# State space operators of a hybrid layer: products and splits taken from GpSimd to VectorE, and u computed three blocks ahead

## The chip, the cores and the metric

The kernel runs on one core of a Trainium2 chip. The core has a matrix engine (TensorE, PE in the profile, with its weight loads as PEld), a vector engine (VectorE, DVE), a scalar engine (ScalarE, ACT), a general engine (GpSimd, POOL) and an engine that here only issues transfers (SyncE, SP). Each engine takes its instructions in the order of its own queue. The metric is the device time of one execution in microseconds; before the change the median of three runs is 1744.01 us.

## What is computed

The layer has a sequence of 1024 tokens behind 16 meta tokens, width 1024. Cut to what matters here:

```
xn = rmsnorm(h);  q, k, v, u, g_att, g_ssm = split(xn @ w_in)
attn = sliding_window_attention(norm(q), norm(k), v)       # 16 heads, 4 kv heads
y = s5_ssm(u, ...)     # 64 groups of 16 channels, 64 complex states each
ssm = za * sigmoid(zb),  za, zb = split(gelu(y) @ w_glu)
h = h + merge(attn, ssm) @ w_out;  h = h + swiglu(rmsnorm(h))
```

The state space branch works in chunks of T = 8 steps. Per block of 8 groups it needs two operator tables of 128 x 1024 numbers, each a complex product of a power of the state matrix with an input or an output matrix: `bp = GR*XB + GI*YB` and `cp = AR*XC + AI*YC`. The matrix products with fp32 accuracy run in three passes: each weight tile is split into a rounded high part and a rest (`lw = raw - hi`).

## The kernel before

**Norm and k, v.** Eight blocks of x (and the meta tokens) are normed (`norm_T`), transposed and split; the reciprocal root is a chain of 13 small VectorE instructions (`rsqrt`, lines 146 to 160). Then k and v are projected, and k is scaled by its norm (line 287, nine products on GpSimd).

**Small chain.** VectorE computes powers of the state matrix on 128 x 64 tables (AR, AI, GR, GI), lines 305 to 388.

**u.** `u_block(f)` (line 400) projects 128 channels of u: the weight tile is loaded by SyncE, rounded by ScalarE (line 103), its rest is taken by GpSimd (line 104), and TensorE makes three products of 272, 256 and 512 columns with 24 matmuls each. A product's PSUM bank is copied out by ScalarE (272 and 512 columns) or VectorE (256 columns, line 407). Eight transfers write u to memory, and `ut` (line 483) reads it back in another layout.

**Operators.** The loop at line 448 takes eight blocks. Each makes bp and cp (lines 460 to 463: first product on GpSimd into the one buffer `tmp`, second product and sum on VectorE; all three are called `ops` in the trace), writes cp out, multiplies bp into `kl`, transposes it into `bpt`, calls `u_block(blk + 1)`, reads `ut`, multiplies it with `bpt` into `v`, copies that into `vs` and lets `step` (line 187, ten VectorE instructions a block, shown as cm and vs) combine neighbouring chunks. XB, YB, XC and YC come from eight transposes of b and c (`bcT`, line 434) that stand behind `u_block(0)`. XB uses the buffer of the small chain's `t12`.

**After it.** Four gate units (`g_unit`, line 526, 24 matmuls each; their weights are split by `w_cols` on GpSimd) and the attention follow. The attention's buffers take the memory that the operators' pool `pp` gives back, the gates' `sg` that of `po`, whose first buffer is YC. The order within each engine's queue is not the written one: a planner simulates the program with its own costs and puts down, at each point, the first written instruction that is ready by its reckoning.

Of the kernel before, what the change touches and what calls it, by code (L numbers as in the profile page):

```python
# [8 lines left out]
F32 = mybir.dt.float32  # L9
F32R = mybir.dt.float32r  # L10
I32 = mybir.dt.int32
BF16 = mybir.dt.bfloat16
AF = mybir.ActivationFunctionType
ALU = mybir.AluOpType
# [3 lines left out]
P = 128  # L18
# [5 lines left out]
HD = 64  # L24
NQ = 16
NKV = 4
# [4 lines left out]
EPS = 1e-6  # L31
# [15 lines left out]
def hybrid_layer_kernel(ctx: ExitStack, tc: tile.TileContext, x, meta_tokens, norm_mix, w_in, q_norm, k_norm,  # L47
                        attn_sinks, lam_re, lam_im, log_dt, ssm_b_re, ssm_b_im, ssm_c_re, ssm_c_im, ssm_d,
                        w_glu, attn_branch_norm, ssm_branch_norm, w_out, norm_ffn, w_ffn_in, w_ffn_out, out):
    nc = tc.nc  # L50
    x, out = x[0], out[0]
# [55 lines left out]
    def w_cols(w, c0, n, name, lo=None, pools=(pool_r,)):  # L107

        per = 1024 // n
        parts = []  # L110
        for i in range(KB // per):
            src = w[i * per * P:(i + 1) * per * P, c0:c0 + n].rearrange("(a p) n -> p a n", p=P)
            parts.append(w_tile(src, (per, n), f"{name}_{i}", lo, pools[i % len(pools)]))
        return lambda kb, part: parts[kb // per][part][:, kb % per, :]
# [31 lines left out]
    def rsqrt(ms, rows, n, pool, name):  # L146

        def t(nm, dt=F32):
            return pool.tile([P, n], dt, tag=f"rs_{nm}{n}", name=f"rs_{nm}_{name}")[:rows]
        xe, xh, q, i = t("xe"), t("xh"), t("q"), t("i", I32)  # L150
        nc.vector.tensor_scalar(out=xe, in0=ms, scalar1=EPS, scalar2=None, op0=ALU.add)
        nc.vector.tensor_scalar(out=xh, in0=ms, scalar1=EPS, scalar2=-0.5, op0=ALU.add, op1=ALU.mult)
        nc.vector.tensor_scalar(out=i, in0=xe.bitcast(I32), scalar1=1, scalar2=None, op0=ALU.logical_shift_right)
        nc.vector.tensor_scalar(out=i, in0=i, scalar1=-1.0, scalar2=float(0x5F3759DF), op0=ALU.mult, op1=ALU.add)
        y = i.bitcast(F32)
        for _ in range(3):
            nc.vector.tensor_tensor(out=q, in0=y, in1=y, op=ALU.mult)
            nc.vector.tensor_tensor(out=q, in0=q, in1=xh, op=ALU.mult)
            nc.vector.scalar_tensor_tensor(out=y, in0=q, scalar=1.5, in1=y, op0=ALU.add, op1=ALU.mult)
        return y  # L160

    def norm_T(src, rows, gain, emit, pool, name, bufs=2):


        ss = pool.tile([P, 1], F32, tag="ss", name=f"ss_{name}")
        xs = pool.tile([P, D], F32, tag="xs", bufs=bufs, name=f"xs_{name}")
        nc.scalar.activation(out=xs[:rows], in_=src[:rows], func=AF.Square, scale=1.0 / 32, accum_out=ss[:rows])
        r = rsqrt(ss[:rows], rows, 1, pool, name)
        nc.vector.scalar_tensor_tensor(out=xs[:rows], in0=src[:rows], scalar=r, in1=gain[:rows],
                                       op0=ALU.mult, op1=ALU.mult)  # L170
        for i in range(2):
            pt = bank(f"nt_{name}_{i}", "x")
            for k in range(4):
                nc.tensor.transpose(pt[:, k * P:k * P + rows], xs[:rows, (4 * i + k) * P:(4 * i + k + 1) * P],
                                    ident[:rows, :rows])
            emit(i, pt.rearrange("p (k n) -> p k n", k=4)[:, :, :rows])
# [37 lines left out]
    with sbuf("p1", 2) as p1:  # L214
# [34 lines left out]
        dt = sm("dt")  # L249
# [34 lines left out]
        kr = rsqrt(kss.rearrange("p b h -> p (b h)"), P, 36, p1, "k").rearrange("p (b h) -> p b h", b=9)  # L284
        for b, (k, n) in enumerate([(ks[:, b, :], P) for b in range(8)] + [(ksm, NMETA)]):
            k = k.rearrange("p (h d) -> p h d", d=HD)
            nc.gpsimd.tensor_tensor(out=k, in0=k, in1=kr[:n, b].unsqueeze(2).to_broadcast([n, NKV, HD]), op=ALU.mult)

        nc.vector.memset(vm.bitcast(F32), 0.0)
        split(vm[0:16, :, 0], vm[0:16, :, 1], o[:NMETA, 256:512].rearrange("p (h d) -> p h d", d=HD))  # L290
# [2 lines left out]
        def tt(o, a, b, op=ALU.mult, eng=None):  # L293
            (eng or nc.vector).tensor_tensor(out=o, in0=a, in1=b, op=op)  # L294
# [31 lines left out]
        dt = sh  # L326
# [63 lines left out]

    def xn_cols(w, c0, name, emit):

        wt = w_cols(w, c0, P, name)
        for h, off, n in ((0, 0, 272), (0, 272, 256), (1, 0, 512)):
            o = bank(f"{name}_{h}_{off}")
            mm3(o[:, :n], wt, lambda kb, part: xn[h][part][:, kb, off:off + n], KB)
            emit(o[:, :n], off + 528 * h, n)

    with sbuf("pp", 1) as pp:
        def u_block(f):  # L400
            uf = pp.tile([P, T, NCH], F32, tag="uf", bufs=2, name=f"uf{f}")

            def emit(o, c0, n):
                dst = uf.rearrange("p t n -> p n t")[:, c0 // T:(c0 + n) // T, :]
                src = o.rearrange("p (n t) -> p n t", t=T)
                if n == 256:
                    nc.vector.tensor_copy(dst, src)  # L407
                else:
                    nc.scalar.copy(dst, src)
            xn_cols(w_in, CU + f * P, f"u{f}", emit)  # L410
            for t in range(T):
                nc.sync.dma_start(out=u_d[f, :, t], in_=uf[:, t, :])
# [8 lines left out]
        nc.gpsimd.memset(zrows, 0.0)  # L421
        nc.gpsimd.dma_start(out=kl_d[8:15].rearrange("s c g e -> (s c) (g e)"), in_=zrows)

        u_block(0)

        XB, YB, XC, YC = (po.tile([P, 16, GRP], F32, tag=n, name=n) for n in ("XB", "YB", "XC", "YC"))
        for what in range(2):
            raw = bc[what][:GRP].rearrange("g a b -> g (a b)")
            X, Y = ((XB, YB), (XC, YC))[what]
            for hh in range(2):  # L430
# [6 lines left out]
                def half(v):  # L437
# [4 lines left out]
                                        scalar2=None, op0=ALU.mult)  # L442
        ops = [pp.tile([P, 2, D], F32, tag="bc", bufs=2, name=f"ops{i}") for i in range(2)]
        bp, cp = (ops[0][:, i].rearrange("p (g s c) -> p g s c", g=8, s=8) for i in range(2))
        tmp = ops[1][:, 0].rearrange("p (g s c) -> p g s c", g=8, s=8)
        bpts = ops[1][:, 1], pp.tile([P, D], F32, tag="bpt", name="bpt1")
        SH = [P, 8, 8, 16]
        for blk in range(8):
            g0 = blk * 8
            bpt = bpts[blk % 2]  # L450

            def gs(v):
                return v[:, :, g0:g0 + 8].rearrange("p s g -> p g s").unsqueeze(3).to_broadcast(SH)

            def cs(v):
                return v[:, :, g0:g0 + 8].rearrange("p c g -> p g c").unsqueeze(2).to_broadcast(SH)

            dd = pp.tile([P, P], F32, tag="dd", name=f"dd{blk}")
            nc.scalar.dma_start(out=dd, in_=ssm_d[0:1, g0 * 16:g0 * 16 + P].to_broadcast([P, P]))
            for o, (p1_, q1), (p2_, q2) in ((bp, (GR, XB), (GI, YB)), (cp, (AR, XC), (AI, YC))):  # L460
                tt(tmp, gs(p1_), cs(q1), eng=nc.gpsimd)
                tt(o, gs(p2_), cs(q2))
                tt(o, o, tmp, ALU.add)
            nc.sync.dma_start(out=cp_d[blk], in_=cp.rearrange("p g t c -> p (g t c)"))
            kl = bank(f"kl{blk}", "x")
            for g in range(8):
                nc.tensor.matmul(kl[:, g * 16:g * 16 + 16], bp[:, g].rearrange("p s c -> p (s c)"),
                                 XC[:, :, g0 + g], start=True, stop=True)
            for hh in range(2):
                pt = bank(f"bpT{blk}{hh}", "x")  # L470
                for g in range(4):
                    nc.tensor.transpose(pt[:, g * P:g * P + P], bp[:, hh * 4 + g].rearrange("p s c -> p (s c)"), ident)
                nc.scalar.copy(bpt[:, hh * 512:hh * 512 + 512], pt)
            kls = pp.tile([P, 8, 16], F32, tag="kls", bufs=2, name=f"kls{blk}")
            tt(kls, dd.rearrange("p (g c) -> p g c", c=16),
               ident[:, 112:128].unsqueeze(1).to_broadcast([P, 8, 16]))
            tt(kls, kls, kl[:, 0:128].rearrange("p (g c) -> p g c", c=16), ALU.add)
            nc.sync.dma_start(out=kl_d[0:8, :, g0:g0 + 8, :].rearrange("s c g e -> (s c) g e"), in_=kls)
            if blk < 7:
                u_block(blk + 1)  # L480

            ut = pp.tile([P, 8, NCH], F32, tag="ut", bufs=2, name=f"utv{blk}")
            nc.sync.dma_start(out=ut, in_=u_d[blk].rearrange("g t c n -> (t c) g n"))
            vs = pp.tile([P, 2, 4, NCH], F32, tag="vs", bufs=2, name=f"vs{blk}")
            for e in range(2):
                for j in range(2):
                    o = bank(f"v{blk}{e}{j}", "q" if j else "x")
                    for k in range(2):
                        g = e + 4 * j + 2 * k
                        nc.tensor.matmul(o[:, k * NCH:(k + 1) * NCH], bpt[:, g * P:g * P + P], ut[:, g, :],  # L490
                                         start=True, stop=True)
                    for ri in range(2):
                        nc.scalar.copy(vs[64 * e:64 * e + 64, ri, 2 * j:2 * j + 2, :],
                                       o[64 * ri:64 * ri + 64, 0:2 * NCH].rearrange("p (k n) -> p k n", k=2))


            step(vs[:, :, :, 1::2], vs[:, :, :, 0::2], a8, 4 * blk, pp)
            step(vs[:, :, :, 5::4], vs[:, :, :, 3::4], a16, 4 * blk, pp)
            nc.sync.dma_start(out=v_d[:, :, 4 * blk:4 * blk + 4, :], in_=vs)
# [268 lines left out]
    for c in range(5, NCH - 1, 4):  # L768
        s1 = W[:, :, :, c]
        nc.vector.tensor_tensor(out=m, in0=W[:, :, :, c - 4].unsqueeze(1).to_broadcast([P, 2, 2, GRP // 2]),  # L770
                                in1=a32.rearrange("p (k r) g -> p k r g", k=2), op=ALU.mult)
# [508 lines left out]
```

## Time and profile before

| | |
|---|---|
| median of 3 runs (lowest, highest) | 1744.01 us (1743.16, 1745.96) |
| profiled execution, time | 1743.45 us |
| profiled execution, span of the trace | 1741.7 us |
| mean granted TensorE clock | 0.959 of full speed |
| busy: PE, DVE, ACT, POOL | 1599.2, 1203.1, 692.3, 510.1 us |

The span runs from the first to the last instruction, and the execution's time is 1.75 us longer. Busy shares are means over the whole span; the stage that the change touches lies between 70 and 286 us of it.

### The profile page before, as it was taken

The page shows a single profiled execution, that of the slowest core. Times are in us where ns is not written, and L with a number is a line of the kernel's source. Part 1 is how long each engine was busy: PE and PEld are TensorE (multiplying, and loading weights), DVE is VectorE, ACT ScalarE, POOL GpSimd, SP SyncE. Part 2 cuts the span into 40 slices and gives each one's busy share as a digit, 9 for nine tenths or more (in the row PEclk, how much of TensorE's full clock was granted, in tenths as well). Part 3 has the DMA queues.
Part 4 walks back from the last instruction along what each step waited for, and adds up shares of the span by engine and source line. Part 5 has one row for each costly group of instructions (what it writes and reads, how often), then busy time and mean ns, then how long its engine had stood idle before and what let it go on. Part 6 is the DMA issues. An engine that isn't in the chain of part 4 may idle for free.

```text
span 1741.7 us, 22246 instructions
## 1 busy us (share of the span) xinstructions
PE 1599.2 (92%) x8002; PEld 1331.6 (76%) x8002; DVE 1203.1 (69%) x2247; ACT 692.3 (40%) x1355; POOL 510.1 (29%) x345
## 2 busy tenths in 40 slices
PE   7968899989989968889999798799999999799998
PEld 5767788868767857788888687688888888678887
DVE  7779983899996699552114768966665556299763
ACT  4323233888886311153222332533333333244330
POOL 0245431333242523401332400012111111256541
PEclk9988899999999988989999999899999999999999
DMA  5153443110111853492221343233333222395432
GB/s 185 46 112 107 133 147 102 31 38 27 36 49 46 288 159 97 128 272 67 73 73 55 120 152 116 73 121 107 100 109 103 91 92 79 128 348 182 145 111 78
DMA packets 175358, 196.93 MB, mean 113 GB/s; under 512 B 12768, under 2 KB 125408, under 8 KB 175120
## 3 DMA queue, kind: packets, MB, share of 16 engines
q1 hardware_dynamic: 166736, 183.94, 32.8%
q10 hardware_dynamic: 8288, 11.01, 2.0%
q8 instruction: 63, 1.03, 0.3%
q0 software_dynamic: 224, 0.56, 0.1%
q14 instruction: 47, 0.39, 0.1%
HBM read 140.62 MB, written 54.85 MB: 112 GB/s over the span
## 4 chain that ended last, share of the span: by engine, by line
PE 61%; DVE 25%; DMA 6%; issue 5%; ACT 2%; POOL 1%; SPq 1%; ACTq 0%; DVEq 0%; POOLq 0%
PE ch_fg L891 6%; PE ch_fu L891 6%; PE ch L891 5%; PE za L122 5%; PE wo L122 5%; PE zb L122 5%; PE si L891 4%; PE th_fg L891 3%; PE th_fu L891 3%; PE q L122 2%; PE kv L122 2%; PE g L122 2%; DVE cm L192 2%; DVE pr L649 2%; DVE ops L294 2%
## 5 line engine op out<-in xcount | busy, mean ns | idle before, releaser
L122 PE MATMUL g<-xn,wh_g 128*128 128x512 f32 x512 | 162.9, 398 | 1.2 <-DVE av L712 1.0
L891 PE MATMUL ch<-B,A 128*128 128x512 f32 x528 | 127.0, 397 | 10.5 <-ACT B L1212 7.8
L891 PEld LDWEIGHTS ch<-B,A 128*128 128x128 f32 x528 | 100.5, 192 | 34.3 <-ACT B L1212 8.2
L122 PEld LDWEIGHTS g<-xn,wh_g 128*128 128x128 f32 x512 | 96.7, 190 | 24.5 <-DVE av L712 1.2
L122 PE MATMUL u<-xn,wh_u 128*128 128x272 f32 (+2 forms) x384 | 96.7, 344 | 13.5 <-DVE uf L407 13.5
L895 POOL TENSOR_TENSOR a<-c,c_fg 128x512 f32<-128x512 f32 x10 | 15.9, 1586 | 315.0 <-DVE c L895 211.0
L122 PE MATMUL g<-xn,wl_g 128*128 128x512 f32 x256 | 101.9, 398 | 0.0
L122 PE MATMUL q<-wh_q,xn 128*128 128x256 f32 x512 | 101.4, 287 | 0.0
L891 PE MATMUL si<-B,A 128*128 128x512 f32 x396 | 92.5, 389 | 0.0
L122 PE MATMUL wo<-wh_o,mt 128*128 128x512 f32 x256 | 83.1, 403 | 9.3 <-DVE h L968 4.9
L891 PEld LDWEIGHTS si<-B,A 128*128 128x128 f32 x396 | 74.3, 188 | 15.5
L122 PEld LDWEIGHTS u<-xn,wh_u 128*128 128x128 f32 x384 | 69.5, 205 | 19.7 <-DVE uf L407 13.7
L842 DVE TENSOR_TENSOR ssm<-za,zs 128x512 f32<-128x512 f32 x16 | 11.0, 690 | 105.4 <-ACT zs L841 105.4
L122 PEld LDWEIGHTS q<-wh_q,xn 128*128 128x128 f32 x512 | 82.4, 191 | 1.2 <-issue 0.5
L122 PE MATMUL zb<-zt,wh_zb 128*128 128x512 f32 x256 | 79.3, 390 | 0.0
L122 PE MATMUL za<-zt,wh_za 128*128 128x512 f32 x256 | 79.2, 390 | 0.0
L1212 ACT CAST A<-rawa 128x1536 fp32r<-128x1536 f32 (+1 forms) x28 | 38.4, 1373 | 97.0 <-issue 44.2
L895 POOL TENSOR_TENSOR B<-t,B 128x1536 fp32r<-128x1536 f32 (+1 forms) x16 | 61.4, 3849 | 50.0 <-ACT B L1212 50.0
L122 PE MATMUL q<-wl_q,xn 128*128 128x256 f32 x256 | 73.2, 286 | 0.0
L895 DVE TENSOR_TENSOR A<-rawa,A 128x1536 fp32r<-128x1536 f32 (+1 forms) x28 | 63.3, 2261 | 13.4 <-ACT A L1212 13.4
L655 ACT ACTIVATE pr<-pr,mn 128x272 f32<-128x272 f32 (+1 forms) x128 | 64.9, 507 | 17.7 <-DVE mn L649 14.6
L122 PE MATMUL u<-xn,wl_u 128*128 128x272 f32 (+2 forms) x192 | 65.6, 343 | 0.0
(428 smaller groups left out, 4386.0 us busy)
## 6 DMA issues: line engine op xcount, KB each, us to landing
rawa<-act_d SPq DMA_DIRECT2D x21, 768.0 KB
raw_fg<-in_w_ffn_in_dram SPq DMA_DIRECT2D x20, 512.0 KB
raw_fu<-in_w_ffn_in_dram SPq DMA_DIRECT2D x20, 512.0 KB
rawb<-in_w_ffn_out_dram SPq DMA_DIRECT2D x6, 1536.0 KB
act_d<-a SPq DMA_DIRECT2D x33, 256.0 KB
raw_g<-in_w_in_dram SPq DMA_DIRECT2D x16, 512.0 KB
act_d<-c_fg SPq DMA_DIRECT2D x30, 256.0 KB
u_d<-uf SPq DMA_DIRECT2D x64, 65.0 KB
```

The lines of the kernel that those rows point to most:

```text
L122: nc.tensor.matmul(o, lhs(kb, a), rhs(kb, b), start=(kb == 0 and i == 0), stop=(kb == n - 1 and i == 2))
L192: nc.vector.tensor_tensor(out=m, in0=v, in1=a[:, 2 * k:2 * k + 2, g0:g0 + 4].unsqueeze(3) .to_broadcast([P, 2, 4, n]), op=ALU.mult)
L294: (eng or nc.vector).tensor_tensor(out=o, in0=a, in1=b, op=op)
L649: nc.vector.tensor_tensor_reduce(out=pr[:, h, :n], in0=o[:, :n], in1=mask, scale=1.0, scalar=nsink[:, kv * 4 + h:kv * 4 + h + 1], op0=ALU. ...
L655: nc.scalar.activation(out=pr[:, h, :n], in_=pr[:, h, :n], func=AF.Exp, scale=-1.0, bias=mn[:, h:h + 1], accum_out=den[:, h:h + 1])
L842: nc.vector.tensor_tensor(out=dst, in0=oa, in1=sg, op=ALU.mult)
L891: nc.tensor.matmul(o, lhs(kb, a), rhs(kb, b), start=(first and kb == 0 and i == 0), stop=(kb == n - 1 and i == 2), skip_group_check=not first)
L895: eng.tensor_tensor(out=out, in0=in0, in1=in1, op=op)
L1212: nc.scalar.copy(hi, src)
```

## The change

Four edits of engine or order. (1) `norm_T` uses `rsqrt1`, a chain of ten instructions in place of 13. (2) k's scaling, the weight rests of u and the first products of bp and cp go from GpSimd to VectorE. (3) The copy of u's 256-column product goes from VectorE to ScalarE. (4) Three blocks of u are written before the transposes of b and c, and the loop then calls `u_block(blk + 3)`. The gates' and q's weight rests stay on GpSimd.

```
+    def rsqrt1(ms, rows, pool, name):
...
+        nc.vector.tensor_scalar(out=xe, in0=ms, scalar1=EPS, scalar2=None, op0=ALU.add)
+        nc.vector.tensor_scalar(out=i, in0=xe.bitcast(I32), scalar1=1, scalar2=None, op0=ALU.logical_shift_right)
+        nc.vector.tensor_scalar(out=xh, in0=xe, scalar1=-0.5, scalar2=None, op0=ALU.mult)
+        nc.vector.tensor_scalar(out=i, in0=i, scalar1=-1.0, scalar2=float(0x5F3759DF), op0=ALU.mult, op1=ALU.add)
+        y = i.bitcast(F32)
+        for _ in range(3):
+            nc.vector.scalar_tensor_tensor(out=q, in0=y, scalar=xh, in1=y, op0=ALU.mult, op1=ALU.mult)
+            nc.vector.scalar_tensor_tensor(out=y, in0=q, scalar=1.5, in1=y, op0=ALU.add, op1=ALU.mult)
...
-        r = rsqrt(ss[:rows], rows, 1, pool, name)
+        r = rsqrt1(ss[:rows], rows, pool, name)
...
-            nc.gpsimd.tensor_tensor(out=k, in0=k, in1=kr[:n, b].unsqueeze(2).to_broadcast([n, NKV, HD]), op=ALU.mult)
+            nc.vector.tensor_tensor(out=k, in0=k, in1=kr[:n, b].unsqueeze(2).to_broadcast([n, NKV, HD]), op=ALU.mult)
...
-        wt = w_cols(w, c0, P, name)
+        wt = w_cols(w, c0, P, name, nc.vector)
...
-                if n == 256:
-                    nc.vector.tensor_copy(dst, src)
-                else:
-                    nc.scalar.copy(dst, src)
+                nc.scalar.copy(dst, src)
...
-        u_block(0)
+        AHEAD = 3
+        for f in range(AHEAD):
+            u_block(f)
...
-                tt(tmp, gs(p1_), cs(q1), eng=nc.gpsimd)
+                tt(tmp, gs(p1_), cs(q1))
...
-            if blk < 7:
-                u_block(blk + 1)
+            if blk + AHEAD < 8:
+                u_block(blk + AHEAD)
```

## Rows read from the trace of the kernel before

**Rows 1.** Busy time by stage: PE, PEld, DVE, ACT, POOL, then clock and DMA share.

```profile
70.00:102.00 32.00, 19.39 (x118) 15.35 (x116) 31.41 (x85) 10.44 (x16) 19.29 (x15) 0.87 0.45 101
102.00:286.00 184.00, 161.00 (x943) 145.57 (x944) 148.86 (x147) 59.17 (x111) 70.89 (x27) 0.88 0.44 128
286.00:560.00 274.00, 253.72 (x1698) 212.07 (x1698) 239.86 (x760) 218.50 (x607) 96.58 (x146) 0.97 0.14 40
```

**Rows 2.** Who waited for whom, 100 to 290 us: total, times, longest.

```profile
ACT wh_g L103 <- DVE kls L294: 25.2, 2, 15.8
PE u L122 <- DVE uf L407: 13.5, 1, 13.5
PE v L490 <- DMA utv<-u_d: 13.3, 4, 4.1
```

**Rows 3.** VectorE's timeline, 99 to 286 us: start, duration, instruction, idle before.

```profile
112.32 0.69 DVE L440 TENSOR_SCALAR YB<-bcT 64x512 f32<-64x512 f32 x1 [9.49 <-ACT XB L439]
113.74 2.30 DVE L294 TENSOR_TENSOR kls<-dd,ident 128x128 f32<-128x128 f32 x1
...
118.92 0.63 DVE L407 COPY uf<-u 128x256 f32<-128x256 f32 x1
...
131.88 4.37 DVE L294 TENSOR_TENSOR ops<-GI,YB 128x1024 f32<-128x1024 f32 x1
...
168.39 1.95 DVE L294 TENSOR_TENSOR ops<-AI,YC 128x1024 f32<-128x1024 f32 x1
170.26 0.70 DVE L195 TENSOR_TENSOR vs<-vs,cm 128x520 f32<-128x520 f32 x1
...
250.10 3.33 DVE L294 TENSOR_TENSOR ops<-ops,ops 128x1024 f32<-128x1024 f32 x1
...
258.94 0.70 DVE L192 TENSOR_TENSOR cm<-vs,a 128x520 f32<-128x520 f32 x1 [3.33 <-ACT vs L493]
...
264.23 0.38 DVE L198 TENSOR_TENSOR vs<-vs,cm 128x128 f32<-128x128 f32 x1
279.88 0.70 DVE L192 TENSOR_TENSOR cm<-vs,a 128x520 f32<-128x520 f32 x1 [15.28 <-ACT vs L493]
...
285.17 0.39 DVE L198 TENSOR_TENSOR vs<-vs,cm 128x128 f32<-128x128 f32 x1
```

**Rows 4.** GpSimd's timeline, 113 to 253 us, same columns.

```profile
113.26 2.64 POOL L294 TENSOR_TENSOR ops<-GR,XB 128x1024 f32<-128x1024 f32 x1 [9.60 <-ACT XB L439]
119.03 2.39 POOL L104 TENSOR_TENSOR wl_u<-raw_u,wh_u 128x1024 fp32r<-128x1024 f32 x1 [3.13 <-ACT wh_u L103]
...
131.85 2.63 POOL L294 TENSOR_TENSOR ops<-GR,XB 128x1024 f32<-128x1024 f32 x1 [1.34 <-DVE ops L294]
...
249.65 2.70 POOL L104 TENSOR_TENSOR wl_q<-raw_q,wh_q 128x1024 fp32r<-128x1024 f32 x1 [1.80 <-DMA raw_q<-in_w_in_dram]
```

**Rows 5.** VectorE's timeline of one norm chain, first and last instruction.

```profile
7.25 0.15 DVE L151 TENSOR_SCALAR rs_xe_x<-ss_x 128x1 f32<-128x1 f32 x1 [5.49 <-ACT xs_x L167]
...
9.36 0.16 DVE L159 SCALAR_TENSOR_TENSOR rs_i_x<-rs_q_x,rs_i_x 128x1 f32<-128x1 f32 x1
```

**Rows 6.** Line 104's groups: engine, count, ns minimum/median/maximum, first and last start.

```profile
L104 POOL TENSOR_TENSOR wl_u<-raw_u,wh_u x8: 2328/2403/2585, 71.7 to 162.2; 128x1024 fp32r<-128x1024 f32 x8
...
L104 DVE TENSOR_TENSOR wl_kv<-raw_kv,wh_kv x4: 1215/1216/1219, 10.8 to 14.8; 128x1024 fp32r<-128x1024 f32 x4
```

**Rows 7.** TensorE's timeline: u's first matmuls and one 256-column part.

```profile
74.79 1.11 PE L122 MATMUL u<-xn,wh_u 128*128 128x272 f32 x6
...
121.63 0.40 PE L122 MATMUL u<-xn,wh_u 128*128 128x256 f32 x2
...
124.43 0.63 PE L122 MATMUL u<-xn,wh_u 128*128 128x512 f32 x2
```

**Rows 8.** The chain that ended last, in order of time.

```profile
263.52 6.48 DMA utv<-u_d
...
278.88 5.57 PE g L122 x24
```

More of the change, by code (lines that the diff above doesn't have):

```diff
@@ L160, in rsqrt, with t @@
         return y
+    def rsqrt1(ms, rows, pool, name):
+        def t(nm, dt=F32):
+            return pool.tile([P, 1], dt, tag=f"rs_{nm}1", name=f"rs_{nm}_{name}")[:rows]
+        xe, xh, q, i = t("xe"), t("xh"), t("q"), t("i", I32)
+        nc.vector.tensor_scalar(out=xe, in0=ms, scalar1=EPS, scalar2=None, op0=ALU.add)
[6 more added lines that the diff above has]
+            nc.vector.scalar_tensor_tensor(out=y, in0=q, scalar=1.5, in1=y, op0=ALU.add, op1=ALU.mult)
+        return y
     def norm_T(src, rows, gain, emit, pool, name, bufs=2):
```

## The prediction

> **What bounds the kernel now.** I read the busy time by stage first. From 102 to 286 us VectorE is busy 148.9 of 184.0 us and TensorE 161.0 at a granted clock of 0.88 of full speed [rows 1]. Both look full, so the waits decide. In VectorE's own timeline the queue runs without a pause worth naming from 112.32 to 264.61 us: explicit idle times add up to 8.3 us over these 152.3, so it is occupied for 144.0. Then it stands for 15.28 us before its last step, which ends at 285.56 [rows 3]. That last wait is not VectorE's fault: the chain of waits shows the read of u (utv) landing 6.5 us after its issue at 263.52, behind the last u block's writes, then gate units, and q's projection only behind the last of them, at 278.88 + 5.57 = 284.45 [rows 8]. The attention can't begin sooner, since its buffers lie where the operators' pool was. So the end of this stage at 285.6 is what the change can move, and within it VectorE's queue.
>
> The reader is to see next why that queue is so full. At 131.85 GpSimd begins a product, and VectorE's own product at 131.88 lasts 4.37 us [rows 3, 4]; the same shape a few blocks on lasts 1.95 [rows 3]. In the whole stretch 22 VectorE instructions are stretched, from the kls product of 2.30 us at 113.74 to a sum of 3.33 at 250.10 [rows 3], by 1.3 to 2.4 us each over unstretched ones of their shape, together 45.7 us, and every one runs beside one of the 23 GpSimd instructions from 113.26 to 249.65 [rows 4]. I ascribe 32.2 us to the 16 products (15 stretches, 2.15 each; beside the sixteenth GpSimd was the one that waited), 5.9 to three splits of u's weights, and 7.6 to four splits of the gates' and q's, which stay.
>
> **The change, part by part.**
>
> *Products to VectorE.* Removed: 32.2 us of stretching. Added: 16 products. Their shape is that of the products VectorE already does, and start to start one takes 168.39 to 170.26, 1.87 us [rows 3]: 29.9 us. Bounds: 1.2 (a split of the same size with plain operands [rows 6]) to 2.0 us, so 19 to 32. I take 1.87, as layout and size are the same. GpSimd's wait for VectorE before each product goes too, but nothing on VectorE waited long for it, so that is worth nothing by itself.
>
> *Splits of u's weights to VectorE.* 1.22 us each on VectorE against 2.40 on GpSimd [rows 6], some 1.13 start to start. Five of the eight fall into the stage (u blocks 3 to 7): plus 5.7, minus the 5.9 of stretching. The first three fall before 102 us. Each now queues on VectorE behind its cast on ScalarE; if the cast is late, products and steps stand behind the split, and the transposes and v matmuls wait for those. GpSimd's wait for the cast at 119.03 was 3.13 us [rows 4]; I take nothing, as the planner can put the split late, and keep the 3.13 for the range.
>
> *Copies to ScalarE.* Seven copies after 112 us leave VectorE, 0.63 us each by their row [rows 3], about 0.45 start to start: minus 3.2. ScalarE is busy 59.2 of 184 us [rows 1] and covers eight copies of some 0.7 us; without that cover they would cost 5.6. The larger effect is earlier: TensorE stood 13.5 us for the one copy that queued behind VectorE's small chain [rows 2]. What is late next is u itself.
>
> *Three blocks ahead.* A 256-column part of u takes 121.63 to 124.43, 2.80 us [rows 7]; scaled by columns (1040 in all) a block is 11.4 us. TensorE starts u at 74.8 [rows 7]; three blocks without the stand end near 109. The transposes of b and c stand behind them, so VectorE's first instruction on them comes near 110, against 112.32 now [rows 3]. I take 110 and keep 100 (the planner lets the transposes through between two parts) and 116 (u waits for weights) as bounds. Moved with u are its weight loads and 64 writes on SyncE's queue: each block's read of u now has three blocks' time, so the 13.3 us that v waited for it [rows 2] and the 15.28 before the last step go. The writes pass the queue ahead of cp and v writes as before, at the same count.
>
> *k's scaling, the first three splits, the shorter chain.* k's nine products have a quarter of the columns of the 1.22 to 1.87 us above, so 0.3 to 0.5 each; with three splits of 1.13 they add 6 to 8 us to VectorE before the transposes, and take GpSimd's stretching away there. VectorE idled 9.49 us before 112.32 [rows 3], which covers them: nothing. Without that cover they would cost up to 8. A norm chain is 13 instructions from 7.25 to 9.52 us, 0.19 from start to start [rows 5]; three fewer take 0.6 from the first block, which the first matmul waits for. The other eight chains are hidden behind k and v matmuls. Bounds 0 to 1.5; I take 0.6.
>
> **Sum.** VectorE's work from the transposes to the end: 144.0 + 5.7 (the last step) - 32.2 - 5.9 - 3.2 + 29.9 + 5.7 = 144.0 us. So it is no lighter; what goes is the waiting around it. From 110, with the old 8.3 us of idle time kept, it ends at 262.3 instead of 285.6, 23.3 us earlier. With 0.6 in front that is 23.9 off the profiled execution's 1743.45 (its span is 1741.7; the 1.75 around it stay), or 1719.6; the median of the runs is 0.56 above that execution, so 1720.
>
> *A rule weighed.* The rows show a stretch of 2.15 us per GpSimd product of 2.6 us [rows 3, 4]. The Trainium skill (SBUF — State Buffer, Who interferes with whom) says that a VectorE instruction with two SBUF inputs and a GpSimd one that reads SBUF block each other for the whole instruction. Taken at its word with 2.6 us for 16 products, 41.6 us would go in place of 32.2, and the sum would be near 1711; the stretches as measured stay in mine.
>
> **The rivals.**
>
> *The gates don't move forward.* Four gate units take 5.57 us each [rows 8], 22.3 in all. Their results go into memory that YC gives back, and YC is read until the last block's products, some 10 us before the stage's end. If TensorE takes them only then, q starts about 13 us after VectorE is done: a gain of 10 in place of 23.3, 1733. For it: one of them stands right before q in the chain now [rows 8]. Against: their weights are ready early, there are four banks, and with u done by about 195 us TensorE has little else to do.
>
> *VectorE's queue stands at the splits* (slower). Each of the five splits can stop the products behind it. ScalarE's casts of gate weights stood 25.2 us in two waits, behind a VectorE result [rows 2]. From 4.7 us a split on the gain of 23.3 is gone; at 9.4, the smaller of those two (25.2 less 15.8), 47 us are added and the time is 1767. For it: an in-order queue. Against: four weight pairs fit ahead, and u runs three blocks early.
>
> *GpSimd ran beside VectorE for nothing* (slower). If the stretches have another cause, 38.1 us stay and the additions come on top: the end is 300.4, 14.8 later, 1758. Against it: 22 stretches and none without a GpSimd instruction beside it. The Trainium skill (Perfetto Trace Analysis, Optimizing Scalar/DVE Operations) says that with a saturated VectorE moving work to ScalarE or even GpSimd may make sense, and adds that the shared port may spoil it. By its first half this change would be slower; the rows bear out the second.
>
> *More than forecast.* The transposes pass early (100) and idle time falls below 2 us: a gain of 40, 1704.
>
> *It comes out even.* The planner's new order gives the gain away in the attention, where VectorE is busy 239.9 of 274 us [rows 1]: within 0.2%, 1744.
>
> **How the numbers follow.** Forecast 0.60; gates late 0.17; more 0.06; even 0.05; queue at the splits 0.09; stretches stay 0.03. Faster is the first three, slower the last two. Within 0.2% (3.5 us) is what a measurement here can't tell from no change. Faster 0.83, same 0.05, slower 0.12. The forecast's own range is 1702 to 1730 (start 100 to 116, idle 0 to 12). With the late gates and part of the larger gain 1700 to 1739 holds about 8 in 10.
>
> **What would show it.** No VectorE instruction of the operators above 2.1 us except beside four to six gate and q splits; first YB instruction between 100 and 116 us; v without waits for utv; last step before 272; q's matmuls from about 260; the attention stage as long as now (274 us). The prediction is wrong if VectorE shows waits of several us before its u splits, if the gates still stand between the last step and q, or if the attention grows by as much as the operators shrink.

## The result, and the profile after

After the change the median of four runs is 1724.30 us (1721.11 to 1730.69), against 1743.59 (1742.86 to 1745.96) before: ratio 0.9892, 95% interval [0.9862, 0.9922], 19.3 us faster. The prediction was 1720, range 1700 to 1739. The profiled execution is the slowest of the four: 1730.69 us, span 1728.9, so it gains 12.8 us on the profiled execution before (1743.45).

In the changed kernel line numbers are up by 15 (294 is 309, 440 is 454, 192 is 207). Its busy time by stage, in the columns of [rows 1]:

```profile
70.00:102.00 32.00, 30.10 (x173) 25.78 (x172) 29.95 (x102) 11.68 (x18) 0.00 (x0) 0.89 0.67 146
102.00:286.00 184.00, 163.20 (x1034) 148.12 (x1033) 146.53 (x174) 67.89 (x133) 24.75 (x16) 0.92 0.42 125
286.00:560.00 274.00, 252.90 (x1621) 208.60 (x1620) 233.56 (x739) 215.81 (x596) 93.94 (x136) 0.96 0.16 48
```

TensorE works through 70 to 102 us (30.10 against 19.39); GpSimd is down from 70.89 to 24.75 us between 102 and 286. VectorE's timeline, in answer to [rows 3]:

```profile
96.39 0.69 DVE L454 TENSOR_SCALAR YB<-bcT 64x512 f32<-64x512 f32 x1
...
105.03 0.29 DVE L309 TENSOR_TENSOR kls<-dd,ident 128x128 f32<-128x128 f32 x1 [3.54 <-DMA dd<-in_ssm_d_dram]
...
115.38 1.23 DVE L104 TENSOR_TENSOR wl_u<-raw_u,wh_u 128x1024 fp32r<-128x1024 f32 x1 [8.91 <-ACT wh_u L103]
116.52 2.03 DVE L309 TENSOR_TENSOR ops<-GI,YB 128x1024 f32<-128x1024 f32 x1
...
208.82 3.39 DVE L309 TENSOR_TENSOR ops<-ops,ops 128x1024 f32<-128x1024 f32 x1
...
254.40 0.70 DVE L207 TENSOR_TENSOR cm<-vs,a 128x520 f32<-128x520 f32 x1 [3.53 <-ACT vs L507]
...
262.39 1.12 DVE L207 TENSOR_TENSOR cm<-vs,a 128x520 f32<-128x520 f32 x1 [2.29 <-ACT vs L507]
...
268.19 0.39 DVE L213 TENSOR_TENSOR vs<-vs,cm 128x128 f32<-128x128 f32 x1
```

Three things are to be seen. The transposes pass at 96.39 instead of 112.32, but the first product that needs GI and YB begins only at 116.52, behind a split of u's weights that stood 8.91 us for its cast. Of the 22 stretched instructions five are left in the stage, each beside a split of gate or q weights on GpSimd, such as the sum at 208.82:

```profile
208.38 2.74 POOL L104 TENSOR_TENSOR wl_q<-raw_q,wh_q 128x1024 fp32r<-128x1024 f32 x1 [17.85 <-ACT wh_q L103]
```

And the 15.28 us before the last step are 2.29. (dd is a small tensor loaded for each block into one buffer; kls is its product with the identity, to which a part of kl is added, and is written out to kl_d.) The stage ends at 268.58, 17.0 us earlier than 285.56; the attention's last sum, 567.7 before, comes at 550.7, 17.0 earlier too. So the stage's gain is passed on unchanged to the end of the attention. Behind it, in lines that the change does not touch, this execution takes 1178.2 us to the end of its span against 1174.0 before, and 4.2 of the 17.0 are lost there. The median's 19.3 comes from executions of which there is no trace.

ScalarE's and TensorE's timelines show why the split stood:

```profile
114.29 1.05 ACT L103 CAST wh_u<-raw_u 128x1024 fp32r<-128x1024 f32 x1 [4.70 <-PE u L122]
```

```profile
114.42 1.21 PE L448 MATMUL bcT<-ident,bc 64*128 64x64 f32 x16
```

The cast, for the seventh block of u, waits for TensorE, which still reads the weight buffer that it is to fill: TensorE has only then finished the third block of u, and the transposes for XC follow at 114.42. VectorE's queue is in order, and the split was put ahead of the product.

### The profile page after: what moved, and what is told of

It is laid out like the page before. It is cut to its first block, busy times and chain, and to the rows that moved or that the text cites. A ratio compares the mean times of both kernels' runs of the same rounds, so it can differ in the third digit from the quotient of the medians.

```text
span 1728.9 us, 22182 instructions
## 1 busy us (share of the span) xinstructions
PE 1594.5 (92%) x8002; PEld 1326.6 (77%) x8002; DVE 1200.3 (69%) x2245; ACT 696.6 (40%) x1363; POOL 438.4 (25%) x312
## 4 chain that ended last, share of the span: by engine, by line
PE 50%; DMA 4%; DVE 4%; issue 1%; POOL 1%; ACT 1%; SPq 0%; ACTq 0%; POOLq 0%
PE ch_fg L905 6%; PE ch_fu L905 6%; PE ch L905 5%; PE wo L122 5%; PE za L122 5%; PE zb L122 5%; PE si L905 4%; PE th_fg L905 3%; PE th_fu L905 3%; PE si_fg L905 2%; PE si_fu L905 2%; DMA tp<-kl_d 1%; PE ch_e L905 1%; DMA a<-at_d 1%; DVE ssm L873 1%; DMA rawa<-act_d 1%
## 5 line engine op out<-in xcount | busy, mean ns | idle before, releaser
L122 PE MATMUL q<-wh_q,xn 128*128 128x256 f32 x512 | 105.1, 293 | 4.1 <-ACT qp L620 4.1
L122 PE MATMUL u<-xn,wh_u 128*128 128x272 f32 (+2 forms) x384 | 92.4, 333 | 0.0
L104 POOL TENSOR_TENSOR wl_g<-raw_g,wh_g 128x1024 fp32r<-128x1024 f32 x16 | 43.4, 2715 | 178.5 <-ACT wh_g L103 172.7
L905 PEld LDWEIGHTS si<-B,A 128*128 128x128 f32 x396 | 74.3, 188 | 15.4
L909 DVE TENSOR_TENSOR A<-rawa,A 128x1536 fp32r<-128x1536 f32 (+1 forms) x28 | 76.6, 2734 | 10.7 <-ACT A L1226 10.7
```

Of the source, the lines that this page charges most:

```text
L104: (lo or nc.gpsimd).tensor_tensor(out=lw, in0=raw, in1=hi.bitcast(F32), op=ALU.subtract)
L122: nc.tensor.matmul(o, lhs(kb, a), rhs(kb, b), start=(kb == 0 and i == 0), stop=(kb == n - 1 and i == 2))
L905: nc.tensor.matmul(o, lhs(kb, a), rhs(kb, b), start=(first and kb == 0 and i == 0), stop=(kb == n - 1 and i == 2), skip_group_check=not first)
L909: eng.tensor_tensor(out=out, in0=in0, in1=in1, op=op)
```

## The experiments

All times are medians; each ratio is to the kernel before on the same chip. The table is worked out from VectorE's timelines: from the first YB instruction to the end of the last step, with explicit idle times added up (idle) and the rest (occupied).

| kernel | first YB | occupied | idle | end of the stage | time, us |
|---|---|---|---|---|---|
| before | 112.32 | 149.65 | 23.59 | 285.56 | 1743.6 |
| copies alone | 102.86 | 139.66 | 35.93 | 278.45 | 1742.5 |
| + k's scaling | 101.68 | 136.51 | 37.13 | 275.32 | 1731.8 |
| + short chain | 100.23 | 142.62 | 27.84 | 270.69 | 1729.3 |
| + u's splits | 96.99 | 142.20 | 30.82 | 270.01 | 1725.3 |
| + products (one block ahead) | 96.81 | 139.96 | 23.06 | 259.83 | 1721.4 |
| two blocks ahead | 96.69 | 144.93 | 12.04 | 253.66 | 1710.4 |
| three ahead: the change | 96.39 | 144.79 | 27.40 | 268.58 | 1724.3 |

From the stage's end to the attention's last sum it is 279 to 284 us in each kernel that was run, so the attention follows the end of the stage. Behind that sum the profiled executions take another 1173 to 1181 us, in lines that no edit touches, and each is one of several executions. So what a kernel gains at the stage's end and what it gains in time can lie up to 8 us apart. The kernels did not all run on the same chip, so some differences in time are given by the two ratios as well.

**Three blocks ahead alone, one block ahead, and the products back.** The first theory was that the reads of u, three blocks early, carry the gain.

```
before + only:   AHEAD = 3; for f in range(AHEAD): u_block(f); ... u_block(blk + AHEAD)
```

> The kernel before with three blocks of u ahead and nothing else changed. Theory: most of the gain, 12 to 18 of the 19 us, 1726 to 1732. Rival (the products and splits on VectorE or the copy on ScalarE carry it): under 6 us, 1738 or more.

1746.97 us, ratio 1.0013 [1.0, 1.0026]: no gain. VectorE's timeline:

```profile
114.86 0.65 DVE L407 COPY uf<-u 128x256 f32<-128x256 f32 x1 [11.92 <-PE u L122]
...
128.65 0.69 DVE L442 TENSOR_SCALAR YB<-bcT 64x512 f32<-64x512 f32 x1 [7.25 <-ACT XB L441]
```

Before its last step it waits 5.68 us in place of 15.28, but with the copies still on VectorE its queue stands 11.92 us for a part of u, and the operators start 16 us later.

```
-        AHEAD = 3
+        AHEAD = 1
```

> The changed kernel with one block of u ahead, all else as changed. Theory (the wait for the read of u before the last step, 15.3 us, and the v waits are what went): both come back, 10 to 15 us slower than the changed kernel, 1734 to 1739. Rival (the order of u hardly matters once TensorE no longer stands for the copy): at most 4 us slower, 1728 or less.

1721.44 us, ratio 0.9866 [0.984, 0.9891]: as fast as with three. The theory fell. VectorE's last step still waits:

```profile
254.14 0.70 DVE L207 TENSOR_TENSOR cm<-vs,a 128x520 f32<-128x520 f32 x1 [11.87 <-ACT vs L507]
```

The read of u is issued at 239.34, behind the last block's eight writes from 232.03, and the v matmuls, gate units ahead of some, begin at 246.07: the wait that the prediction named, not gone with one block ahead. So three ahead takes away 11.87 us at the end and must pay about as much elsewhere.

```
-                tt(tmp, gs(p1_), cs(q1))
+                tt(tmp, gs(p1_), cs(q1), eng=nc.gpsimd)
```

> The changed kernel with the 16 first products of bp and cp back on GpSimd; u still three blocks ahead, splits and copies as changed. Theory (the ledger of the prediction: moving the products takes 32.2 us of stretching from VectorE and adds 29.9 us of work, so the move itself is nearly even, and the gain comes from the waits for u): 2 to 6 us slower than the changed kernel, 1726 to 1730, with some 15 VectorE instructions stretched by about 2 us again. Rival (the products on VectorE carry the gain): at least 12 us slower, 1736 or more.

1731.50 us, ratio 0.9926 [0.9903, 0.995]: the products' move is worth 7.2 us with three ahead (5.9 by the two ratios, whose intervals overlap). In VectorE's timeline with them on GpSimd:

```profile
126.79 1.23 DVE L309 TENSOR_TENSOR ops<-ops,ops 128x1024 f32<-128x1024 f32 x1 [2.54 <-POOL ops L309]
...
131.18 2.00 DVE L309 TENSOR_TENSOR ops<-AI,YC 128x1024 f32<-128x1024 f32 x1 [2.71 <-DMA cp_d<-ops]
```

VectorE waits for GpSimd's half of a table, and cp, written out later, delays the next. Occupied it is 135.5 us against 144.8 with the products, idle 42.0 against 27.4: the products are more work for VectorE than the stretching was (by 9.3 us), and what the move gives is 14.6 us of waiting.

**Does GpSimd's reading do the stretching?**

```
-                tt(tmp, gs(p1_), cs(q1))
+                for _ in range(3):
+                    nc.gpsimd.memset(tmp, 0.0)
```

> The changed kernel with the 16 first products left out: in their place GpSimd fills the same buffer with zeros three times, about as long as a product took it, so it writes the on-chip memory and reads nothing, and bp and cp are the second products alone. Theory (VectorE is held by GpSimd's reads): no VectorE instruction of the operators above 2.1 us beside the fills, VectorE 30 us lighter than in the changed kernel, the last step 10 us earlier or more. Rival (any GpSimd instruction beside it stretches VectorE): stretches of about 2 us each as before, last step no earlier than with the products on GpSimd.

1702.01 us (two runs), ratio 0.9756 [0.9722, 0.9789]. GpSimd's timeline, then VectorE's:

```profile
123.00 2.98 POOL L476 MEMSET ops<- 128x1024 f32 x3 [27.37 <-DVE ops L309]
...
184.53 4.01 POOL L104 TENSOR_TENSOR wl_q<-raw_q,wh_q 128x1024 fp32r<-128x1024 f32 x1
```

```profile
122.86 2.02 DVE L309 TENSOR_TENSOR ops<-AI,YC 128x1024 f32<-128x1024 f32 x1
...
186.38 4.03 DVE L309 TENSOR_TENSOR ops<-GI,YB 128x1024 f32<-128x1024 f32 x1
```

The kernel leaves out the 16 first products, and the zeros that GpSimd writes into their buffer stand in for its work. The product at 122.86 lasts 2.02 us beside a group of memsets of 2.98; the one at 186.38 lasts 4.03 beside a split, which reads. Between 100 and 246 us just five VectorE instructions exceed 2.1 us, each beside one of the gate and q splits, none beside a group of memsets alone. This is the rule of the Trainium skill (SBUF — State Buffer, Who interferes with whom): two-input VectorE work contends with a GpSimd instruction that reads SBUF, not with one that only writes; the trace agrees. The occupied time, 115.7 us, is 29.1 below that of the change: 1.82 us for each of the 16 products left out, the prediction's 1.87.

**The copies alone, and the splits and k's scaling added to them.**

```
before + only:   nc.scalar.copy(dst, src)     # all three parts of u
```

> The kernel before with the 256-column copies of u on ScalarE and nothing else changed. New theory (the gain is the earlier start: TensorE no longer stands for the copy behind the small chain, so the transposes of b and c reach VectorE when the chain ends): first YB instruction near 103 instead of 112.3 us and the end of the operators as much earlier, 1733 to 1738. Rival (the chain must also be rid of GpSimd's stretching, or the products moved, before anything is gained): 1741 or more.

1742.50 us over ten runs, ratio 0.9999 [0.9984, 1.0013], though the stage ends 7.1 us earlier and the attention 6.4. In the profiled execution 2.5 us are lost between the attention and the last 220 us and 4.7 in these, in lines that are the same (below, under what was not expected); the ten runs lie between 1736.23 and 1746.78. In time this edit alone is not to be told from none.

```
after with   AHEAD = 1   and   tt(tmp, gs(p1_), cs(q1), eng=nc.gpsimd)
```

> The changed kernel with one block of u ahead and the first products of bp and cp on GpSimd: left of the change are the copies, u's splits, k's scaling and the shorter norm chain. Theory (the products' move is even by the ledger, plus handovers between the two engines): 2 to 5 us slower than one ahead with the products moved (1721.4), 1723 to 1727. Rival (with VectorE never idle the products' move is the larger part): 1732 or more.

1725.31 us, ratio 0.9902 [0.9887, 0.9916]. So without the products and without more blocks ahead most of the gain was there already, and lay in edits that the prediction had costed at some 4 us together (copies 3.2, chain 0.6, splits 0.2, scaling nothing) and an earlier start. Three more runs divide them.

```
the same, and   wt = w_cols(w, c0, P, name)       # u's splits on GpSimd
```

> Kernel after with one u block ahead, the 16 first products and the splits of u's weights on GpSimd: what is left of the change is k's scaling on VectorE, the short norm chain and the copies on ScalarE. Beside the kernel with the copies alone (no change in time, YB's first instruction at 102.9 us, last step begins 278.1) it shows the scaling and the chain; beside the one that also has the splits on VectorE (1725 us, 97.0, 269.6) it shows the splits. In the copies-alone trace VectorE's short instructions of the small chain last 0.6 us in place of 0.18 between 92.6 and 99 us, beside GpSimd's scaling of k, and one lasts 2.89 us beside a split at 99.57. If the scaling carries most of the difference: YB at 98 to 100, the last step at 272 to 275, 1729 to 1734 us. If the splits carry it: YB at 101 to 103, the last step at 276 to 278, 1738 to 1743 us. If neither does by itself and the attention's order does: last step near 274 and a time that does not follow it.

1729.33 us, ratio 0.9915 [0.9892, 0.9938]; the stage ends 0.7 us later than with the splits moved. The splits' move is near even.

```
the same, and   r = rsqrt(ss[:rows], rows, 1, pool, name)     # chain of 13
```

> Kernel before with two edits of the change: the 256-column copies on ScalarE and k's scaling on VectorE. It stands between the kernel with the copies alone (first product with YB at 111.9 us, last step begins 278.1, 1742.5 us) and the one that has the short norm chain as well (105.9, 270.3, 1729.3 us). If the scaling carries the difference, by the stretched short instructions beside it and the transfers and the split that wait behind it on GpSimd: first product with YB at 106 to 108, the last step at 270 to 273, 1729 to 1734 us. If the chain of ten carries it, which starts the small chain 1.0 us sooner: 110 to 112, the last step at 276 to 278, 1739 to 1743 us.

1731.77 us, ratio 0.9915 [0.9898, 0.9933]; first product with YB at 105.9 us, as with the short chain; the last step's last instruction begins at 274.9 (278.1 and 270.3 in the two kernels beside it), between what the two theories had. The copies and k's scaling together bring 11.8 us in time and 10.2 at the stage's end; how it divides between the two depends on which is looked at (1.1 and 10.7 in time, 7.1 and 3.1 at the stage's end). By the two ratios (0.9999 and 0.9915) the scaling is worth some 15 us; of the 12.0 us between the two profiled spans, 4.1 are there at the attention's last sum (561.3 and 557.2) and 7.9 come behind it, in lines that no edit touches. What the scaling does in the stage is shown by GpSimd's and VectorE's timelines of the kernel with the copies alone:

```profile
92.57 6.42 POOL L287 TENSOR_TENSOR ks<-ks,rs_i_k 128x256 f32<-128x256 f32 x8 [8.06 <-DVE rs_i_k L159]
...
99.57 2.33 POOL L104 TENSOR_TENSOR wl_u<-raw_u,wh_u 128x1024 fp32r<-128x1024 f32 x1
```

```profile
94.77 0.60 DVE L303 SCALAR_TENSOR_TENSOR a<-a 128x32 f32<-128x32 f32 x1
...
99.05 2.89 DVE L303 SCALAR_TENSOR_TENSOR a<-a 128x32 f32<-128x32 f32 x1
...
105.70 0.77 DVE L294 TENSOR_TENSOR kls<-dd,ident 128x128 f32<-128x128 f32 x1
111.41 0.29 DVE L294 TENSOR_TENSOR kls<-dd,ident 128x128 f32<-128x128 f32 x1 [4.94 <-DMA dd<-in_ssm_d_dram]
```

and VectorE's with the scaling moved:

```profile
95.55 2.77 DVE L302 TENSOR_TENSOR ks<-ks,rs_i_k 128x256 f32<-128x256 f32 x8
...
99.83 0.17 DVE L318 SCALAR_TENSOR_TENSOR a<-a 128x32 f32<-128x32 f32 x1
...
101.36 0.28 DVE L309 TENSOR_TENSOR kls<-dd,ident 128x128 f32<-128x128 f32 x1
...
105.66 0.29 DVE L309 TENSOR_TENSOR kls<-dd,ident 128x128 f32<-128x128 f32 x1 [1.17 <-DMA dd<-in_ssm_d_dram]
```

On GpSimd the eight scalings take 6.42 us and stretch the end of the small chain next to them, an instruction of 0.17 to 0.60, and the split queued behind them to 2.89. On VectorE they take 2.77, and that split begins at 87.34. The first product with YB comes 6.1 us earlier (105.86 against 111.94), but the stretching is the smaller part of that: YB itself starts only 1.2 us earlier (101.68 against 102.86). The other 4.9 lie behind it. The first kls stands ahead of YB's instructions at 101.36 in the one kernel and behind them at 105.70 in the other; the buffer dd, which it reads, is then loaded again that much later, and the second kls, which stands ahead of the product, waits 1.17 us and 4.94 us for it. That order is the planner's. So that the scaling's move helps is shown; that it helps by ending the stretching is shown for 1.2 us only.

**u's splits back with three blocks ahead.**

```
after with   wt = w_cols(w, c0, P, name)
```

> The changed kernel, three ahead, with u's weight splits back on GpSimd. Theory (the split in VectorE's queue is what stands 8.9 us at 106 us): that stand goes, five splits beside VectorE stretch it by about 2 us each in place of 1.13 of own work, the small chain is stretched as before by some 8 us: between 4 us faster and 2 us slower than the changed kernel, 1720 to 1726, and no wait of VectorE over 4 us before 120 us. Rival (VectorE waits there for the first products' operands in any case): the wait of 9 us stays under another name, 1727 or more.

1725.82 us, ratio 0.9907 [0.989, 0.9923], the stage's end 268.79: nothing gained by freeing VectorE from the split. VectorE's and TensorE's timelines:

```profile
111.00 0.69 DVE L454 TENSOR_SCALAR YB<-bcT 64x512 f32<-64x512 f32 x1 [6.21 <-ACT XB L453]
```

```profile
108.55 2.47 PE L448 MATMUL bcT<-ident,bc 64*128 64x64 f32 x24
```

Here the first 24 transposes stand behind the three blocks of u (the other eight come at 115.57), and the start is 111.0, the prediction's 110. The first product with YB comes at 117.3, against 116.52. So the third block costs its 11 us of TensorE at the front either way, as a stand at the split or as late transposes.

**Two blocks ahead.**

```
-        AHEAD = 3
+        AHEAD = 2
```

> The changed kernel with two blocks of u ahead. Theory (three ahead makes VectorE stand 8.9 us at a split of u whose weight buffer TensorE still holds; one ahead leaves 11.9 us of wait before the last step): two ahead has neither in full, 1712 to 1719. Rival (the wait only moves): 1720 to 1725, as with one or three.

1710.39 us (1708.77 to 1714.13), ratio 0.982 [0.9805, 0.9835], 13.9 us faster than the change (12.6 by the two ratios). VectorE's timeline:

```profile
106.08 2.02 DVE L309 TENSOR_TENSOR ops<-GI,YB 128x1024 f32<-128x1024 f32 x1
...
245.93 0.70 DVE L207 TENSOR_TENSOR cm<-vs,a 128x520 f32<-128x520 f32 x1 [2.53 <-ACT vs L507]
...
253.24 0.42 DVE L213 TENSOR_TENSOR vs<-vs,cm 128x128 f32<-128x128 f32 x1
```

Neither the stand at the split nor the wait at the end. Occupied time is the same as in the change (144.93 and 144.79); idle time is 15.4 us less, the stage ends 14.9 sooner.

```
after with   AHEAD = 2   and   tt(tmp, gs(p1_), cs(q1), eng=nc.gpsimd)
```

> Kernel after with two u blocks ahead and the 16 first products on GpSimd. Two ahead with the products on VectorE took 1710.4 us, with neither the stand at a split of u nor the long wait before the last step. The products' move was worth 3.9 us with one block ahead and 7.2 with three, where part of what it saves was given back in those waits. If the products are worth what the stretches less their own time and the handovers' waits (some 8 us in the three-ahead kernel) give, this kernel takes 1718 to 1722 us. If their move is near even, as the ledger had it (2.3 us saved), 1712 to 1714.

1713.83 us, ratio 0.9833 [0.9802, 0.9863]: the intervals of the two overlap, and the stage ends at 252.34, 1.3 us before the one with the products on VectorE. Occupied 135.48 and idle 20.58 against 144.93 and 12.04: with the products on VectorE 9.5 us more work, 8.5 less waiting. The products' move is near even here.

```
d3 = dd.rearrange("p (g c) -> p g c", c=16)         # two ahead, and:
tt(d3, d3, ident[:, 112:128]...);  tt(kls, d3, kl[:, 0:128]..., ALU.add)
```

> Kernel after with two u blocks ahead, and the product of dd with the identity written into dd itself, so that only the sum of it with kl writes the buffer kls, whose transfer to memory VectorE waits for in the two-ahead kernel (2.79 us at 193.01 and 2.73 at 213.28, three such waits with three ahead). If these waits lie on VectorE's path, the last step ends 3 to 6 us earlier than in the two-ahead kernel (it began at 253.2 there) and the time is 1704 to 1708 us, against 1710.4. If VectorE only meets its next wait sooner, or the sum waits in the product's place, the time stays within 2 us of 1710.

1719.33 us, ratio 0.9859 [0.9838, 0.988]: a miss, 8.9 us slower than two ahead without it (6.8 by the two ratios). VectorE's timeline:

```profile
231.00 0.29 DVE L309 TENSOR_TENSOR dd<-dd,ident 128x128 f32<-128x128 f32 x1 [4.10 <-DMA dd<-in_ssm_d_dram]
```

The wait for kl_d is gone, and four of 2.24 to 4.10 us for the load of dd have come, which now can't start before the sum has read it. Neither theory had that.

## Why the prediction was right in the total, and where its steps were not

**The stage's end bounds the time.** Right as far as the attention: the end of the last step moved by 17.0 us, the end of the attention by 17.0. What lies behind was taken as unchanged, and is 4.2 us longer in the profiled execution.

**Sum.** VectorE's work was forecast as 144.0 us: 144.79 measured. The start was forecast as 110: 96.39, outside the bounds 100 to 116. Idle time was carried over as 8.3: 27.40. So 262.3 became 96.39 + 144.79 + 27.40 = 268.58. The two errors are in the main one: the three blocks of u did hold up the operators for about as long as forecast (first product at 116.52), but as idle time behind transposes that passed early (8.91 of it at the split, 3.54 for dd), and three waits for kl_d (8.3 together) and the 5.8 before the last two steps came on top.

**Three blocks ahead: the step that failed.** It was credited with the end of the waits for utv, and those went. But its own price, a later start, was only set beside the old start (110 against 112.32), where it looks like a gain of 2.3 us, and not beside the start with fewer blocks ahead: the first product with YB comes at 105.49 and 106.08 with one and two, at 116.52 with three. Measured beside two blocks, which take the same waits away, the third costs 15.4 us of VectorE's idle time and 13.9 us of the run.

**The rival that came true in part.** VectorE's queue stood at a split, by the mechanism described, 8.91 us and once, not at five splits; only three splits of u fall into the stage (105.24, 115.38 and 134.86), and the other two did not wait for their casts. It took more than a third of the forecast 23.3 without deciding the sign. What was held against it, that u runs three blocks ahead, was its cause: the cast for the seventh block needs the weight buffer of the third, which TensorE frees only after finishing that block.

**Products.** The saved stretching was taken as 32.2 us and the products as 29.9, net 2.3 for the change. The products' own time was right (1.82 against 1.87 each). The stretching was too large a term for the kernel as changed: with them on GpSimd VectorE is occupied 9.5 and 9.3 us less with two and three blocks ahead, so that some 20 us of stretching go (16 times 1.82, less 9.4). With one block ahead, as in the kernel from which it was read, it is 2.2 us more, as forecast. What was costed at nothing, "nothing on VectorE waited long for it", is worth 7.8 to 14.6 us of idle time. With two and three blocks ahead the waits for GpSimd's half and for cp's write are 9.8 and 10.9 us, against 0.4 and 0.8 with the products on VectorE: all of the difference with two, two thirds of it with three. With one ahead no wait is put down to GpSimd, and how the 7.8 come about is open. The move is worth 3.9, 3.4 and 7.2 us of the run with one, two and three blocks ahead, or 6.3, 2.3 and 5.9 by the ratios; by these only the first is outside the uncertainty.

**Splits of u.** Taken as even (5.7 against 5.9): 4.0 us with one block ahead, 1.5 with three, both with overlapping intervals, the stage's end 0.7 and 0.2 apart. Right within the measurement.

**Copies.** Taken as 3.2 us of work and an earlier start. By themselves they end the stage 7.1 us earlier and bring no time that can be told from none.

**k's scaling.** Costed at nothing, "up to 8" as a loss. Wrong in sign: with the copies it brings 11.8 us where the whole change brings 19.3. The cover that was counted on, VectorE's idle time before YB, is not there either: in the changed kernel YB follows the small chain at once. GpSimd's scalings stretch the short end of that chain, behind which YB stands in VectorE's queue, but that is 1.2 us; 4.9 more come through the order of VectorE's queue and the load of dd, and what the scaling is worth behind the attention has no shown cause.

**Short chain.** 0.6 forecast; 2.4 us in the run, nothing by the two ratios (0.9915 each), so not settled.

**The other rivals.** GpSimd beside VectorE for nothing: no, by the memsets. Late gates: no, q's first matmul comes at 259.2, 9 us ahead of the last step's end. The attention takes as long as before (282.1 us from the stage's end, as before).

That the total came within 4.3 us is partly luck. Inside the sum the start came 13.6 us early and idle time 19.1 us high; seen by edits, a gain that was put too low (k's scaling and the copies) and a price that was put too low (the third block) work against each other. The profiled execution, for which the sum was made, was forecast at 1719.6 and took 1730.69: its stage ends 6.9 us later than forecast (262.3 less 0.6 for the chain), and 4.2 are lost behind the attention. The median lies closer because the other three executions were faster than the profiled one; where they gained is not shown.

## What to carry to other kernels

Ask of every buffer's lead what it costs at the front and take the smallest that removes the wait: two blocks did what three did and were 13.9 us faster. Look for a second engine's interference also beside short chains of dependent instructions, and then check how much of the later gain it explains: here 1.2 of 6.1 us, and the order of a queue the rest. When work is moved off an engine that slows its neighbour, count three things: here, with three blocks ahead, some 20 us of stretching and 14.6 of waiting go, and 29 us of own work come.

## What was not expected of the hardware

The same stretching goes with 4 to 5 us at the end of the run, in code that no edit touched. In the profiled execution of the copies alone, GpSimd's, VectorE's and TensorE's timelines and a window (columns of [rows 1]) show:

```profile
1612.22 3.50 POOL L892 TENSOR_TENSOR B<-t,B 128x1536 fp32r<-128x1536 f32 x1 [2.69 <-ACT B L1209]
```

```profile
1612.26 5.07 DVE L892 TENSOR_TENSOR A<-rawa,A 128x1536 fp32r<-128x1536 f32 x1
```

```profile
1622.04 10.09 PE L888 MATMUL ch<-B,A 128*128 128x512 f32 x36 [3.50 <-DVE h2o L892]
```

```profile
1620.00:1630.00 10.00, 7.96 (x28) 6.41 (x29) 7.62 (x8) 0.33 (x1) 4.32 (x1) 0.83 0.53 200
```

A weight rest that takes 1.75 us at 1619.64 in the same trace takes 5.07 when it begins 0.04 us after GpSimd's; TensorE then stands 3.50 us before 1622.04, and its mean granted clock from 1620 to 1630 is 0.83 of full speed. The three executions in which TensorE stands these 3.50 us (copies alone, products back with three and with two ahead) spend 225.5 to 226.0 us from the first ch matmul to the end of the span, the others 220.4 to 222.5. A long rest alone does not do it: the changed kernel's execution has two (5.06 us at 1612.24, 5.05 at 1622.95), TensorE stands at most 1.4 us for one thing there once these matmuls run, and it spends 222.5. So which of the two engines starts first goes with the length of the rest, and where TensorE waits for it, it is enough to hide a gain of 5 us. Whether the planner set these queues in the same order in all kernels is not shown.
